# An encoder layer in split fp32: all instructions recorded and issued in a planned order, 8 KB tiles in shared places, whole-block operand parts, six of eight pairs in seven products

## The chip, the cores and the metric

The kernel runs on one core of one Trainium2 chip. The metric is the device time of one execution in microseconds (us), and the median of several runs counts. A core has a matrix engine (TensorE, "PE" in the profile; "PEld" is its weight load), a vector engine (VectorE, "DVE"), a scalar engine (ScalarE, "ACT"), GpSimd ("POOL") and a sync engine ("SP") that here only issues DMAs. Each engine works its own instructions off in order and waits on semaphores for the others. Matmuls write to PSUM, eight banks of 128 x 512 fp32; everything else lies in SBUF, 128 partitions wide.

## The reference

One encoder layer for 256 tokens of width 2048, in fp32:

```python
x = x + 0.5 * swiglu(rmsnorm(x, ffn1_norm), ffn1_w_gate, ffn1_w_up, ffn1_w_down)
h = rmsnorm(x, mix_norm)
proj = h @ w_in                          # pool | q | k | v | q_mem | gate logits, 12800 columns
gates = sigmoid(proj[..., c5:] + b_gate)
y_pool = pooling_branch(u_pool, pool_w, pool_scale) @ w_up_pool
y_attn = dilated_attention_branch(q, k, v, positions) @ w_up_attn
y_mem = memory_branch(q_mem, rmsnorm(mem, mem_norm), w_mem_kv) @ w_up_mem
merged = gates_0 * y_pool + gates_1 * y_attn + gates_2 * y_mem
x = x + merged @ w_out
x = x + 0.5 * swiglu(rmsnorm(x, ffn2_norm), ffn2_w_gate, ffn2_w_up, ffn2_w_down)
return rmsnorm(x, final_norm)
```

`swiglu(x, g, u, d)` is `(silu(x @ g) * (x @ u)) @ d` with 5632 hidden columns. The two FFNs hold most of the weights.

## The kernel before

**Split fp32.** Every fp32 operand is split into a high part (rounded to the matrix engine's fp32r format by a ScalarE copy, line 112) and a low part (the rest, by a VectorE subtraction, line 113). A product of two blocks takes three matmuls: low x high, high x high, high x low (lines 207 to 209 in `gemm`, 232 to 234 in `pair_gemm`, 597 to 599 in the down products). Each has a stationary block of 128 x 128 (the activations) and a moving block of 128 x 512 (the weights).

**Weights.** `weights` (line 130) loads four 128-row blocks of 512 columns in one DMA of 1 MB into a tile `wf` (three of them). `kept` (line 121) splits it in two halves of two blocks: one ACT copy and one DVE subtraction of 128 x 1024 for each half, into the 4 KB tiles `wh` and `wl`, of which there are six each. `pair_weights` does the same for a pair of row blocks of the gate matrix (`n` = 0) and of the up matrix (`n` = 1), in two DMAs of 512 KB; for the first pair of the first chunk it loads and splits block by block (`piece` = 1).

**The FFN.** `ffn` goes over 11 chunks of 512 hidden columns (`up(c)`). A chunk multiplies the 16 row blocks of the width, as eight *pairs* j = 0 to 7, with the gate and the up matrix. A pair is a 2 x 2 block product: two token blocks by two row blocks, times two row blocks by (gate, up). Done plainly it takes eight products (`EIGHT_PRODUCTS`); with sums of blocks on both sides it takes seven (`SEVEN_PRODUCTS`, a Strassen-Winograd scheme). `SEVEN = (1, 2, 3, 5, 6)` lists the pairs that do; in chunk 0 none do, in chunk 1 those in `SEVEN[1::2]` (2 and 5), in chunks 2 to 10 all five, and these come first in the chunk. A seven-product pair needs sums of weight blocks: three VectorE additions (lines 155 to 157; the first is 128 x 1024), then a split of the four sums (lines 160 and 161), and its own three blocks are split too (`kept(wf, 3)`). It needs sums of the activation blocks as well, once per FFN, from `fill_pair`. The products add up in one PSUM bank each, and `finish` combines them when the last pair is done.

From chunk 2 on, the down product of chunk c - 2 is put between the seven-product products: eight pieces of 12 matmuls (`down_pieces`), one PSUM bank, then an ACT copy to a tile `y` (line 601, two `half` places, shared with other small tiles) and a POOL DMA that adds `y` to x in DRAM (line 602, `accum_op`). The down products of the last two chunks are done as plain gemms at the end, and x is loaded back by `x_chunk` (line 546).

**The middle.** After FFN 1 come plain gemms (`gemm`, two sets of two PSUM banks in turn) for the memory keys, values and queries, the pooling input, the gates, q, k, v, the up projections and `w_out`, with the small work of the branches put between them.

**What sets the order.** The program itself is written in the order wanted: `queue` holds small pieces of work (transposes, splits, activations), and `pop` sets some of them in after each product. Each engine's instructions then follow that writing order as the tile framework schedules it, with waits where a tile's place isn't free yet. SP issues nearly all loads, in order, and POOL the stores of x.

**Memory.** A pool of 14 `slot` places of 8 KB (per partition) holds operands, sums and the larger tiles; beside it lie three `wf` of 8 KB, six `wh` and six `wl` of 4 KB. An FFN's activations take five `seven` tiles and two shared `lhs` tiles for the other three pairs.

**The start.** SP issues the loads of the transposed x (`load_x`, 256 KB a pair) between those of the weights. Nine idle matmuls warm TensorE. For pair 1 (`SUMS = {5: 1}`) the sums of activation blocks are made later, before pair 5 of chunk 1 (`late_sums`); for the other seven-product pairs at once.

Of the kernel before, what the change touches and what calls it, by code (L numbers as in the profile page):

```python
# [9 lines left out]
F32 = mybir.dt.float32  # L10
# [32 lines left out]
SEVEN = (1, 2, 3, 5, 6)  # L43
SUMS = {5: 1}
# [21 lines left out]

@with_exitstack
def tile_encoder_layer(ctx: ExitStack, tc: tile.TileContext, a: dict, out: bass.AP):
    nc = tc.nc
    sb = ctx.enter_context(tc.tile_pool(name="sb", bufs=1))  # L70
    ps = ctx.enter_context(tc.tile_pool(name="ps", bufs=1, space=bass.MemoryType.PSUM))
    dr = ctx.enter_context(tc.tile_pool(name="dr", bufs=1, space=bass.MemoryType.DRAM))
# [6 lines left out]
    def slot(shape, dtype=F32, name="slot"):  # L79
        return sb.tile(shape, dtype, tag="slot", bufs=14, name=nm(name))  # L80
# [49 lines left out]
    def weights(w, row, col):  # L130

        wf = sb.tile([P, 4, CW], F32, tag="wf", bufs=3, name=nm("wf"))
# [3 lines left out]
    def pair_weights(w, cols, j, seven, piece=2, beside=()):  # L136


        wf = sb.tile([P, 4, CW], F32, tag="wf", bufs=3, name=nm("wf"))
        beside = list(beside)  # L140
        halves = [operands() for _ in range(2)] if piece < 2 else None
        for n in range(2):
            block = w[n][cols[n] // CW, j // 2].rearrange("p (k c) -> p k c", k=4)
            for k in range(0, 2, piece):
# [4 lines left out]
                if piece < 2:  # L149
                    wh, wl = halves[n]  # L150
                    split(wh[:, k : k + 1], wl[:, k : k + 1], wf[:, r])
        if not seven:
            return halves or kept(wf, 4)
# [29 lines left out]
    def gemm(lhs, w, row, col, last=False, sets=((0, 1), (2, 3))):  # L183
# [10 lines left out]
        for pairs in order:  # L194
            for kb, t in pairs:
# [7 lines left out]
                wh, wl = W[kb // 4][kb // 2 % 2]  # L203
# [3 lines left out]
                nc.tensor.matmul(parts[t], lo, wh[:, k % 2], start=kb == 0, stop=False)  # L207
                nc.tensor.matmul(parts[t], hi, wh[:, k % 2], start=False, stop=False)  # L208
                nc.tensor.matmul(parts[t], hi, wl[:, k % 2], start=False, stop=kb == n - 1)  # L209
# [13 lines left out]
    def pair_gemm(lhs, w, cols, order, sevens, out, after_seven=(), before=None, pieces=None, between=()):  # L223
# [12 lines left out]
        def block(W, b):  # L236

            wh, wl = W[min(b // 2, 2)]
            i = b - 4 if b >= 4 else b % 2
            return wh[:, i], wl[:, i]  # L240
# [938 lines left out]
```

## Time and profile before

| what | value |
|---|---|
| median of 3 runs (lowest to highest) | 2348.73 us (2348.28 to 2348.74) |
| profiled execution | 2348.81 us, span 2347.0 us |
| TensorE clock granted, mean | 0.999 |
| VectorE, FFN chunks (140 to 620 us) | 419.59 us busy of 480 |
| ScalarE, the same | 295.73 us busy of 480 |
| DMA, the same | 77% of the 16 engines, 227 GB/s |
| VectorE, the middle (740 to 1600 us) | 594.08 us busy of 860 |

The span goes from the first to the last instruction; the execution's time has 1.8 us around it. A row of the grouped view names line, engine, operation, tiles (out <- in), shape and count; then the total busy time, the mean of one, and the idle time of the engine just before these instructions with what ended it. A row of the timeline begins with the start and the duration in us, and "x2" joins neighbours; what stands in brackets is idle time before it and its releaser. A window's row gives, for PE, PEld, DVE, ACT and POOL, busy us and (instructions), then the clock, the DMA share and GB/s.

### The profile page before, as it was taken

How to read it: one execution, taken by the hardware profiler on the slowest of the kernel's cores; microseconds unless marked ns; L12 is line 12 of the kernel's file. 1: busy time of each engine (PE TensorE's matmuls, PEld its weight loads, DVE VectorE, ACT ScalarE, POOL GpSimd, SP SyncE). 2: the span in 40 equal slices, each digit the busy share in tenths (PEclk: the TensorE clock that was granted, in tenths of full speed). 3: DMA queues.
4: the chain of work that ended last, by engine and by line, in shares of the span. 5: the costliest groups of instructions: out<-in, count | busy, mean ns of one | idle time of the engine just before them, and what ended most of it. 6: DMA issues, size and time to landing. Idle time of an engine off the chain costs nothing.

```text
span 2347.0 us, 27962 instructions
## 1 busy us (share of the span) xinstructions
PE 2334.9 (99%) x10271; PEld 1877.0 (80%) x10271; DVE 1827.2 (78%) x2218; ACT 1311.8 (56%) x1609; POOL 138.5 (6%) x174
## 2 busy tenths in 40 slices
PE   9999999999999999999999999999999999999998
PEld 7888888888888888888888888887887888888886
DVE  7988888889867676757777656876698988888875
ACT  8565666666566445543334454455566666565654
POOL 0011111111100000000000000000011111111110
PEclk9999999999999999999999999999999999999999
DMA  8687878777786545555545455566577777777883
GB/s 327 207 237 217 248 229 236 222 228 223 229 294 223 197 180 198 188 199 187 188 180 197 171 173 189 202 218 207 195 213 226 229 228 225 229 220 223 245 253 147
DMA packets 119033, 506.27 MB, mean 216 GB/s; under 512 B 13680, under 2 KB 14960, under 8 KB 87664
## 3 DMA queue, kind: packets, MB, share of 16 engines
q1 hardware_dynamic: 95952, 459.39, 56.7%
q0 software_dynamic: 22656, 44.05, 10.7%
q8 instruction: 80, 1.31, 0.2%
q10 hardware_dynamic: 288, 1.05, 0.1%
q14 instruction: 57, 0.47, 0.1%
HBM read 458.30 MB, written 46.14 MB: 215 GB/s over the span
## 4 chain that ended last, share of the span: by engine, by line
PE 99%; DMA 0%; DVE 0%; SPq 0%; ACT 0%; issue 0%; DVEq 0%; ACTq 0%
PE acc L208 13%; PE acc L207 13%; PE acc L209 13%; PE q L232 13%; PE q L233 13%; PE q L234 13%; PE down L598 6%; PE down L599 6%; PE down L597 6%; PE bank L396 1%; PE bank L877 0%; PE bank L803 0%; PE bank L768 0%; DMA wf<-in_ffn_w_gate 0%; PE bank L861 0%; PE bank L1027 0%
## 5 line engine op out<-in xcount | busy, mean ns | idle before, releaser
L113 DVE TENSOR_TENSOR wl<-wf,wh 128x1024 fp32r<-128x1024 f32 (+1 forms) x834 | 951.9, 1159 | 362.8 <-ACT wh L112 358.8
L112 ACT ACTIVATE wh<-wf 128x1024 fp32r<-128x1024 f32 (+1 forms) x834 | 837.1, 1009 | 702.9 <-PE acc L208 406.1
L207 PE MATMUL acc<-wh,lhs 128*128 128x512 f32 x1344 | 537.7, 400 | 0.0
L208 PE MATMUL acc<-wh,lhs 128*128 128x512 f32 x1344 | 534.3, 398 | 0.0
L209 PE MATMUL acc<-wl,lhs 128*128 128x512 f32 x1344 | 528.4, 393 | 0.0
L207 PEld LDWEIGHTS acc<-wh,lhs 128*128 128x128 f32 x1344 | 252.5, 188 | 64.7 <-DVE lhs L113 0.3
L209 PEld LDWEIGHTS acc<-wl,lhs 128*128 128x128 f32 x1344 | 252.3, 188 | 60.6
L208 PEld LDWEIGHTS acc<-wh,lhs 128*128 128x128 f32 x1344 | 252.7, 188 | 54.3
L160 ACT ACTIVATE sumsh<-sums 128x1024 fp32r<-128x1024 f32 x188 | 197.0, 1055 | 105.9 <-DVE sums L157 58.3
L161 DVE TENSOR_TENSOR sumsl<-sums,sumsh 128x1024 fp32r<-128x1024 f32 x188 | 228.1, 1220 | 11.2 <-ACT sumsh L160 10.3
L598 PE MATMUL down<-wh,lhs 128*128 128x512 f32 x576 | 228.5, 397 | 0.0
L599 PE MATMUL down<-wl,lhs 128*128 128x512 f32 x576 | 228.0, 396 | 0.0
L597 PE MATMUL down<-wh,lhs 128*128 128x512 f32 x576 | 227.5, 395 | 0.0
L232 PE MATMUL q<-wh,lhs 128*128 128x512 f32 x528 | 222.1, 421 | 2.1 <-ACT wh L112 2.1
L233 PE MATMUL q<-wh,lhs 128*128 128x512 f32 x528 | 208.3, 395 | 0.0
L234 PE MATMUL q<-wl,lhs 128*128 128x512 f32 x528 | 208.2, 395 | 0.0
L602 POOL DMA_DIRECT2D x<-y x144 | 124.6, 865 | 1156.6 <-ACT y L601 1136.3
L232 PE MATMUL q<-wh,seven 128*128 128x512 f32 x410 | 163.9, 400 | 0.0
L234 PE MATMUL q<-wl,seven 128*128 128x512 f32 x410 | 162.5, 397 | 0.0
L601 ACT ACTIVATE y<-down 128x512 f32<-128x512 f32 x144 | 85.3, 592 | 138.1 <-PE down L599 79.7
L233 PE MATMUL q<-wh,seven 128*128 128x512 f32 x410 | 162.0, 395 | 0.0
L233 PE MATMUL q<-sumsh,seven 128*128 128x512 f32 x376 | 148.7, 395 | 0.0
(174 smaller groups left out, 2551.7 us busy)
## 6 DMA issues: line engine op xcount, KB each, us to landing
wf<-in_w_in SPq DMA_DIRECT2D x100, 1024.0 KB, 4.8
wf<-in_ffn_w_down SPq DMA_DIRECT2D x88, 1024.0 KB, 5.3
wf<-in_ffn_w_gate SPq DMA_DIRECT2D x175, 512.0 KB, 5.3
wf<-in_ffn_w_up SPq DMA_DIRECT2D x175, 512.0 KB, 6.7
x<-y POOLq DMA_DIRECT2D x144, 256.0 KB, 6.4
wf<-in_w_mem_kv SPq DMA_DIRECT2D x16, 1024.0 KB, 5.2
wf<-in_w_out SPq DMA_DIRECT2D x16, 1024.0 KB, 4.8
wf<-in_w_up_pool SPq DMA_DIRECT2D x8, 1024.0 KB, 4.8
```

The source lines that it names most:

```text
L112: nc.scalar.activation(hi, src, AF.Copy)
L113: nc.vector.tensor_sub(lo, src, hi.bitcast(F32))
L161: nc.vector.tensor_sub(tl[:, r], sums[:, r], th[:, r].bitcast(F32))
L207: nc.tensor.matmul(parts[t], lo, wh[:, k % 2], start=kb == 0, stop=False)
L208: nc.tensor.matmul(parts[t], hi, wh[:, k % 2], start=False, stop=False)
L209: nc.tensor.matmul(parts[t], hi, wl[:, k % 2], start=False, stop=kb == n - 1)
L232: nc.tensor.matmul(Q[q], lhsl, wh, start=first, stop=False)
L233: nc.tensor.matmul(Q[q], lhsh, wh, start=False, stop=False)
L234: nc.tensor.matmul(Q[q], lhsh, wl, start=False, stop=final)
L597: nc.tensor.matmul(b, lo, wh[:, k % 2], start=k == 0, stop=False)
L598: nc.tensor.matmul(b, hi, wh[:, k % 2], start=False, stop=False)
L599: nc.tensor.matmul(b, hi, wl[:, k % 2], start=False, stop=k == 3)
```

## The change

1. Every instruction is recorded first (`Recorder`, `Plan.record`), with its tiles, the parts of them that it reads and writes, and an assumed cost. At the end `Plan.issue` plays the program through with these costs: each engine takes, of the instructions whose inputs are ready, the one recorded earliest whose tiles have a place (`room`); SP and POOL keep the recorded order. The instructions are then issued in the order found, and each tile has the place that the play gave it.
2. All 8 KB tiles (`slot`, `wf`, `wh`, `wl`) share 23 places.
3. Operand parts are four blocks wide: `kept` splits a weight tile in one ACT and one DVE instruction. The four sums' low parts are one DVE instruction too; their high parts stay two ACT copies.
4. `SEVEN = (1, 2, 3, 4, 5, 6)`. Chunk 1 has pairs 2, 4 and 6 in seven products, chunks 2 to 10 six pairs. In FFN 1 all sums of activation blocks are made later: their record index is shifted to 220 (pairs 2, 4, 6) or 400 (pairs 1, 3, 5).
5. The loads of `x_chunk`, `mem`, `memT`, `inv_count`, `pool_w`, `b_gate` and `mask` are issued by POOL instead of SP.

The diff, cut to its core (`View` stands for a tile or a part of one and notes slicing and reshaping; `View.bits` gives the cells that it covers):

```diff
-SEVEN = (1, 2, 3, 5, 6)
-SUMS = {5: 1}
+SEVEN = (1, 2, 3, 4, 5, 6)
+SUMS = (220, 400)
...
+    def record(self, engine, name, args, kw):
...
+        for view, writes in [(v, False) for v in views] + [(v, True) for v in outs]:
+            t, bits = view.tile, view.bits()
+            tiles[id(t)] = t
+            for other, theirs, wrote in t.log:
+                chained = engine == other.engine == "tensor"
+                if other is not w and (theirs & bits and (writes or wrote) or chained and writes and wrote):
+                    before.add(other)
...
+        w.index = len(self.works) + self.shift
+        self.works.append(w)
...
+    def cost(self, engine, name, out, views, kw):
+        if name == "dma_start":
+            return (60, 0) if engine != "gpsimd" else (860, 0)
+        n = max(v.free() for v in [out, *views] if isinstance(v, View))
+        if engine == "tensor":
+            if name == "transpose":
+                return 111, 160
+            n = out.free()
+            dtype = views[0].dtype
+            if dtype == F32:
+                return 0.84 * 2 * n, 160
+            return (n * 17 / 16 + 16 if dtype == F32R else n) / 2.4, 160
+        if engine == "vector":
+            if name == "transpose":
+                return 180 + n, 30
+            return (210 if name == "scalar_tensor_tensor" else 160) + 1.042 * n, 30
+        if engine == "scalar":
+            return 210 + 0.834 * n + (50 if any(v.free() <= 2 for v in views) else 0), 30
+        return 500, 100
+
+    def issue(self):
...
+        def room(w):
+            need = {}
+            for t in w.tiles:
+                if t.placed is None:
+                    need.setdefault(id(t.group), (t.group, []))[1].append(t)
+            for group, tiles in need.values():
+                first = min(t.rank for t in tiles)
...
+                earlier = sum(t.placed is None for t in group.tiles[group.next : first])
+                if len(group.free) - earlier < len(tiles):
+                    return False
+            return True
...
+            for e in engines:
+                while free_at[e] <= now and able[e]:
+                    skipped, w = [], None
+                    if e in turn and able[e][0][0] != turn[e][0]:
+                        break
+                    while able[e] and len(skipped) < (1 if e in turn else 24):
+                        item = heapq.heappop(able[e])
+                        if room(item[1]):
+                            w = item[1]
+                            break
+                        skipped.append(item)
...
+                    end = now + w.cost
+                    if w.link and w.link != link:
+                        link = w.link
+                        end += 1283
+                    free_at[e] = end
+                    done = end + w.lag
+                    if w.bytes:
+                        hard = e != "gpsimd"
+                        lines = max(end + (1300 if hard else 2000), lines) + w.bytes / (190 if w.adds else 365)
+                        done = lines + (600 if hard else 1000)
+                    order.append(w)
...
+        with self.tc.manual_schedule():
+            for w in order:
+                w.call()
...
-        return sb.tile(shape, dtype, tag="slot", bufs=14, name=nm(name))
+        return sb.tile(shape, dtype, tag="slot", bufs=23, name=nm(name))
...
     def operands():
-        return [sb.tile([P, 2, CW], F32R, tag=tag, bufs=6, name=nm(tag)) for tag in ("wh", "wl")]
+        return [slot([P, 4, CW], F32R, name) for name in ("wh", "wl")]
 
     def kept(wf, n):
-        halves = [operands() for _ in range(2)]
-        for i, (wh, wl) in enumerate(halves):
-            m = min(2, n - 2 * i)
-            split(wh[:, :m], wl[:, :m], wf[:, 2 * i : 2 * i + m])
-        return halves
+        wh, wl = operands()
+        split(wh[:, :n], wl[:, :n], wf[:, :n])
+        return wh, wl
...
-        wf = sb.tile([P, 4, CW], F32, tag="wf", bufs=3, name=nm("wf"))
+        wf = sb.tile([P, 4, CW], F32, tag="slot", bufs=23, name=nm("wf"))
...
         for r in (slice(0, 2), slice(2, 4)):
             nc.scalar.activation(th[:, r], sums[:, r], AF.Copy)
-            nc.vector.tensor_sub(tl[:, r], sums[:, r], th[:, r].bitcast(F32))
-        return *kept(wf, 3), (th, tl)
+        nc.vector.tensor_sub(tl, sums, th.bitcast(F32))
+        return kept(wf, 3), (th, tl)
...
+            def rest():
+                straight(1)
+                with nc.shifted(max(0, sums_at - nc.now())):
+                    own(0)
+                    own(1)
+                    sums()
+                    parts(slice(4, 8))
+
+            return [lambda: straight(0), rest]
...
-        fill = fill_pair(lhs1[j], lambda: xt, g_ffn1[:, 2 * j : 2 * j + 2], own_only=j in SUMS.values())
+        fill = fill_pair(lhs1[j], lambda: xt, g_ffn1[:, 2 * j : 2 * j + 2], SUMS[j not in SEVEN[1::2]])
...
-            nc.sync.dma_start(out=xs[:, t], in_=XD[n][t])
+            nc.gpsimd.dma_start(out=xs[:, t], in_=XD[n][t])
...
-        nc.sync.dma_start(
+        nc.gpsimd.dma_start(
             out=bg, in_=a["b_gate"][:, i * D + n * CW : i * D + (n + 1) * CW].partition_broadcast(P)
         )
...
+    nc.issue()
```

More of the change, by code (lines that the diff above doesn't have):

```diff
@@ L1 @@
-from contextlib import ExitStack
+from contextlib import ExitStack, contextmanager
 import numpy as np
@@ new lines, with __init__, place @@
+class Whole:
+    def __init__(self, make, group, shape):
+        self.make, self.group, self.shape = make, group, shape
+        self.whole, self.made, self.users, self.log = None, None, 0, []
+        self.placed = None
+    def place(self):
+        if self.made is None:
+            self.made = self.make(self.placed)
+        return self.made
+class Group:
+    def __init__(self, places):
+        self.free, self.tiles, self.next = list(range(places)), [], 0
+class Work:
+    def __init__(self, engine, call, cost, lag):
+        self.engine, self.call, self.cost, self.lag = engine, call, cost, lag
+        self.waits, self.then, self.ready, self.tiles, self.link = 0, [], 0.0, (), 0
+        self.bytes, self.adds = 0, False
@@ L136, in pair_weights @@
     def pair_weights(w, cols, j, seven, piece=2, beside=()):
-        wf = sb.tile([P, 4, CW], F32, tag="wf", bufs=3, name=nm("wf"))
+        wf = sb.tile([P, 4, CW], F32, tag="slot", bufs=23, name=nm("wf"))
         beside = list(beside)
-        halves = [operands() for _ in range(2)] if piece < 2 else None
+        parts = operands() if piece < 2 else None
         for n in range(2):
@@ L149, in pair_weights @@
                 if piece < 2:
[L150 to L151 removed]
+                    split(parts[0][:, r], parts[1][:, r], wf[:, r])
         if not seven:
[L153 removed]
+            return (parts or kept(wf, 4),)
         sums = slot([P, 4, CW], F32, "sums")
@@ L360, in fill_pair, with own, sums, parts @@
             return [lambda k=k: part(k) for k in range(2)]
-        if own_only:
+        F = []
+        def own(k):
+            if not F:
+                F.append(tmp([P, 8, P], "blocks"))
+            nc.scalar.activation(
+                F[0][:, 2 * k : 2 * k + 2], src()[:, k].rearrange("p (t c) -> p t c", t=T), AF.Copy, scale=gain[:, k : k + 1]
+            )
+        def sums():
+            nc.vector.tensor_sub(F[0][:, 4], F[0][:, 3], F[0][:, 1])
+            nc.vector.tensor_sub(F[0][:, 5], F[0][:, 2], F[0][:, 3])
+            nc.vector.tensor_sub(F[0][:, 6], F[0][:, 2], F[0][:, 4])
+            nc.vector.tensor_sub(F[0][:, 7], F[0][:, 0], F[0][:, 6])
+        def parts(r):
+            split(L[:, 0, r], L[:, 1, r], F[0][:, r])
+        if sums_at is not None:
             def straight(k):
@@ L557, in up @@
             opening = c == 0 and first is not None
-            kw = dict(before=first[0], pieces=lambda j: 1 if j == 0 else 2) if opening else {}
-            if c == 1 and first is not None:
-                kw = dict(before=first[1])
+            kw = dict(before=first, pieces=lambda j: 1 if j == 0 else 2) if opening else {}
             out = []
@@ L693, in load @@
                 rows[t] = slot([P, D], F32, "mem")
-                nc.sync.dma_start(out=rows[t], in_=a["mem"][t * P : (t + 1) * P, :])
+                nc.gpsimd.dma_start(out=rows[t], in_=a["mem"][t * P : (t + 1) * P, :])
             else:
                 columns[n] = tmp([P, 4, S], "xt")
-                nc.sync.dma_start(out=columns[n], in_=a["memT"][:, 4 * n : 4 * n + 4, :])
+                nc.gpsimd.dma_start(out=columns[n], in_=a["memT"][:, 4 * n : 4 * n + 4, :])
         def squares(t, n):
@@ L945, in tile_encoder_layer @@
     mask = v2[:, 1]
-    nc.sync.dma_start(out=mask, in_=a["mask"])
+    nc.gpsimd.dma_start(out=mask, in_=a["mask"])
     for g in range(3):
```

234 lines of the change are left out of this document (191 added, 43 removed).

## The prediction

> **What bounds the kernel now.** I read the page first: busy times, then the chain that ended last.
>
> ```profile
> span 2347.0 us, 27962 instructions
> PE 2334.9 (99%) x10271; PEld 1877.0 (80%) x10271; DVE 1827.2 (78%) x2218; ACT 1311.8 (56%) x1609; POOL 138.5 (6%) x174
> PE 99%; DMA 0%; DVE 0%; SPq 0%; ACT 0%; issue 0%; DVEq 0%; ACTq 0%
> L207 PE MATMUL acc<-wh,lhs 128*128 128x512 f32 x1344 | 537.7, 400 | 0.0
> L598 PE MATMUL down<-wh,lhs 128*128 128x512 f32 x576 | 228.5, 397 | 0.0
> L232 PE MATMUL q<-wh,lhs 128*128 128x512 f32 x528 | 222.1, 421 | 2.1 <-ACT wh L112 2.1
> L232 PE MATMUL q<-wh,seven 128*128 128x512 f32 x410 | 163.9, 400 | 0.0
> L233 PE MATMUL q<-sumsh,seven 128*128 128x512 f32 x376 | 148.7, 395 | 0.0
> ```
>
> The chain is TensorE for 99%. "Busy" is no proof, because matmuls overlap (0.40 us listed each), so I take the step from one start to the next out of the timeline of an FFN chunk.
>
> ```profile
> 199.64 0.39 PE L597 MATMUL down<-wh,lhs 128*128 128x512 f32 x1
> ...
> 208.49 0.39 PE L234 MATMUL q<-wl,lhs 128*128 128x512 f32 x1
> 208.72 0.27 PE L396 MATMUL bank<-ident,up 128*128 128x128 f32 x1
> ...
> 209.30 0.39 PE L234 MATMUL q<-wl,lhs 128*128 128x512 f32 x1
> ```
>
> From 199.64 to 208.49 lie 38 steps: 8.85 / 38 = 0.233 us for a 512-column matmul. From 208.49 to 209.30 there are three matmuls and one transpose: 0.81 - 0.70 = 0.11 us for the transpose. Each of the five groups above stands once in each of the three lines of its triple, so there are 3 x (1344 + 576 + 528 + 410 + 376) = 9702 such matmuls, and 9702 x 0.233 = 2261 us. That leaves 86 us of the span for 569 small matmuls (some 0.12 us each: 68 us) and about 18 us for start and tail. So the sum closes with next to no waiting in between: only fewer matmuls, a shorter start or a shorter tail can make it faster, and any stall makes it slower. The start and the tail:
>
> ```profile
> 5.55 0.51 PE L232 MATMUL q<-wh,lhs 128*128 128x512 f32 x1 [0.67 <-ACT wh L112]
> ...
> 6.59 0.62 PE L234 MATMUL q<-wl,lhs 128*128 128x512 f32 x2
> 8.68 0.50 PE L232 MATMUL q<-wh,lhs 128*128 128x512 f32 x1 [1.47 <-ACT wh L112]
> ...
> 9.50 0.41 PE L234 MATMUL q<-wl,lhs 128*128 128x512 f32 x1
> ...
> 12.78 0.39 PE L234 MATMUL q<-wl,lhs 128*128 128x512 f32 x1
> 13.01 0.40 PE L232 MATMUL q<-wh,seven 128*128 128x512 f32 x1
> ```
> ```profile
> 11.56 1.06 ACT L112 ACTIVATE wh<-wf 128x1024 fp32r<-128x1024 f32 x1 [0.35 <-DMA wf<-in_ffn_w_gate]
> 12.81 1.06 ACT L112 ACTIVATE wh<-wf 128x1024 fp32r<-128x1024 f32 x1 [0.18 <-DMA wf<-in_ffn_w_up]
> ```
> ```profile
> 2338.36 0.69 DVE L616 SCALAR_TENSOR_TENSOR xs<-acc,xs 128x512 f32<-128x512 f32 x1
> ```
>
> The first real matmul starts at 5.55; two starts at 6.59 and 6.82 are followed by one at 8.68, a hole of 8.68 - 6.82 - 0.23 = 1.6 us in which the second gate piece is awaited. Pair 1 begins at 13.01, without a hole behind pair 0. The tail, from L616 at 2338.36 to the end, is 8.6 us.
>
> **The change, part by part.**
>
> *Products.* A pair in seven products saves one product of three matmuls. Before, each FFN has 2 such pairs in chunk 1 and 5 in each of chunks 2 to 10: 47, twice 94, which the count below (x94) confirms. After it has 3 and 6: 57, twice 114. Twenty products go, 60 matmuls x 0.233 = **14.0 us**, all of it on the chain. For the vector engine it means more work, below.
>
> *Operand parts four blocks wide.* One ACT and one DVE instruction in place of two. VectorE at saturation, and the widths on both engines:
>
> ```profile
> 212.51 1.22 DVE L155 TENSOR_TENSOR sums<-wf 128x1024 f32<-128x1024 f32 x1
> 213.65 0.68 DVE L113 TENSOR_TENSOR lhs<-bank,lhs 128x512 fp32r<-128x512 f32 x1
> 214.25 0.68 DVE L156 TENSOR_TENSOR sums<-sums,wf 128x512 f32<-128x512 f32 x1
> ```
> ```profile
> L155 DVE TENSOR_TENSOR sums<-wf 128x1024 f32<-128x1024 f32 x94 | 114.6, 1220 | 5.9 <-DMA wf<-in_ffn_w_up 5.8
> L112 ACT ACTIVATE wh<-wf 128x1024 fp32r<-128x1024 f32 x736 | 775.9, 1059 | 673.0 <-PE acc L208 406.1 <-PE q L233 145.9 <-PE down L598 63.1
> L112 ACT ACTIVATE wh<-wf 128x512 fp32r<-128x512 f32 x98 | 61.9, 631 | 29.8 <-PE down L598 10.5 <-PE q L233 7.6 <-ACT gate L572 6.8
> ```
>
> Back to back a 1024-wide VectorE step takes 1.14 us (212.51 to 213.65) and a 512-wide one 0.60. The step per 512 is 0.54, so 2048 should take 2.22 and 1536 1.68: a merged pair saves only 0.06 us there. [...] On ScalarE 1059 - 631 = 428 ns per 512 gives 1.06 + 0.86 = 1.92 us for 2048. In steady state both lie beside the matmuls and cost nothing; the cover is what was prepared ahead. At the start there is no cover. Chunk 0's pairs from the second on are split whole: the split waits for the up half too (landed when ACT takes it at 12.81), then needs 1.92 us, so pair 1 can begin at about 14.8 and not at 13.01: 1.8 us. Its low parts come 2.3 us after that (2.22 and a hand-over), while the four banks can take two matmuls each meanwhile (8 x 0.233 = 1.9): another 0.3 or so. From pair 2 on, a pair is 24 x 0.233 = 5.6 us of matmuls against 1.92 and 2.22 us, and the split is ahead. I take **+2.0 us**. Bounds: below, -1.6, if the new order closes the hole before 8.68; above, +3.8, if the planned order runs each triple to its end, so that the 1.9 us of filling is lost too.
>
> *Order and places.* `Plan.issue` lays every engine's order out from assumed costs; SP and POOL stay in recorded order. Work lacks nothing now, so a better order has only the hole at 8.68 to win, and a wrong one has everything to lose. The 14 slots, 3 `wf` and 12 half-size parts were 184 KB; 23 shared places are the same. I take 0, with the rivals for the upper bound.
>
> *Loads moved from SP to POOL* (`x_chunk`, `mem`, `memT`, `inv`, `pool_w`, `bg`, `mask`). They pass the accumulating stores in POOL's queue:
>
> ```profile
> x<-y POOLq DMA_DIRECT2D x144, 256.0 KB, 6.4
> ...
> xs<-x SPq DMA_DIRECT2D x24, 256.0 KB, 5.3
> ```
> ```profile
> 2299.03 0.80 SPq L546 DMA_DIRECT2D xs<-x  x2
> ...
> 2306.17 1.39 DVE L616 SCALAR_TENSOR_TENSOR xs<-acc,xs 128x512 f32<-128x512 f32 x2
> ```
>
> Of equal size, POOL's take 1.1 us longer, and two of them follow each other, so a chunk of x may come 1 to 3 us later against 7.1 us from issue to first use; the sums wait in PSUM behind it, of which gemms have two sets in turn. I take 0; without that cover it would be up to 3 us in each of 12 places. In exchange, weights no longer queue behind these waits on SP. The tail's instructions are the same: 0, within half a microsecond either way.
>
> *Sum.* The profiled run took 2348.81 us, the runs' median is 2348.73, so it stands for them. 2348.8 - 14.0 + 2.0 = **2336.8 us**.
>
> **Rivals.**
>
> *VectorE becomes the bound in the seven-product phase* (slower). Six pairs at 1.14 + 2 x 0.60 + 2.22 + 1.68 = 6.24 give 37.4 us, four down blocks 4 x 2.22 = 8.9, twelve narrow steps 7.2: 53.5 us, while TensorE has (42 x 3 + 96) x 0.233 = 51.7 us there. If nothing is prepared ahead, 1.8 us are lost in each of 18 chunks: 32 us, so 2369. It is slower than before once more than 12 / 18 = 0.7 us per chunk stays uncovered. The windows of such a chunk speak about it:
>
> ```profile
> 212.00:256.00 44.00, 44.00 (x192) 35.36 (x191) 43.36 (x49) 28.54 (x35) 3.96 (x5) 1.00 0.78 239
> 256.00:271.00 15.00, 15.00 (x66) 12.07 (x65) 8.72 (x10) 7.35 (x10) 2.09 (x3) 1.00 0.86 244
> 140.00:620.00 480.00, 480.00 (x2093) 385.01 (x2092) 419.59 (x459) 295.73 (x350) 49.53 (x58) 1.00 0.77 227
> ```
>
> VectorE (third pair of columns) already works 43.4 of 44 us in that phase, then idles 6 of 15. By the same prices the present phase needs 31.8 + 9.1 + 7.2 = 48.1 us in 201 x 0.233 = 46.8: a deficit of 1.3, which TensorE doesn't feel. After, the eights phase leaves 12.1 - 4.4 = 7.7 us to work ahead, and the mean load goes from 419.6 / 480 = 87% to about 93%. So it is closer, but places, shared by all, should cover 1.8 us. Chance 0.10.
>
> *ScalarE held at `y`* (same or slower). The copy of a down block into one of two `half` places waits for an accumulating store; behind it in ACT's queue stand the weight splits, and for those TensorE waits.
>
> ```profile
> ACT y L601 <- DMA x<-y: 22.6, 18, 3.2
> ```
>
> The plan counts 860 + 2000 + 1380 + 1000 ns for such a store, 5.2 us, against the 6.4 above. If the 22.6 us reached TensorE in whole it would be 2359, half of it 2348. Against it: TensorE feels none of this now, and down blocks come further apart (42 products for eight of them, not 35). Chance 0.09.
>
> *The start costs nothing* and its hole closes: 2348.8 - 14.0 - 1.6 = 2333.2. Against it: the hole waits on a landing that no order changes. Chance 0.06.
>
> *The clock falls at the new hole at the start.* A hole of 1.8 us could send TensorE back to the rate at which it warmed up:
>
> ```profile
> L323 PE MATMUL idle<-idle 128*128 128x512 bf16 x9 | 3.6, 576 | 1.3 <-DVE idle L320 1.3
> ```
>
> Another 3.6 us at half rate would lose 1.8: 2338.6. Against it: after the 1.6 us hole the step from 9.50 to 12.78 is 3.28 / 14 = 0.234, full speed. Chance 0.03. [...]
>
> **How the numbers follow.** Forecast 0.72, VectorE 0.10, `y` 0.09, cheap start 0.06, clock 0.03. The range takes in the bounds of the start (2348.8 - 14.0 with -1.6 and +3.8: 2333.2 to 2338.6), half a microsecond of tail, and the lower third of the `y` case, up to 2345; it leaves out VectorE and most of `y`. A measurement tells about 0.2% (4.7 us) from no change. Faster: 0.72 + 0.06 + 0.03 and 0.02 of `y`: 0.83. Same: 0.05, slower 0.12.
>
> **What the changed profile would show.** Right: 60 matmuls fewer in the groups of the FFN lines, sums x114, the step still 0.233; a start of pair 1 near 14.8 with a hole before it on ACT's split; VectorE near 93% in the FFN windows and TensorE's starts unbroken there. Wrong: TensorE rows with idle time put down to `wl`, `sumsl` or `wh` in chunks 2 to 10 (the VectorE rival), ACT waits at `y` above 22.6 us with TensorE idle beside them, or holes at a gemm's start behind a POOL load.

## The result and the profile after

| | before | after |
|---|---|---|
| median of the runs, us | 2348.73 (2348.28 to 2349.04) | 2307.43 (2305.32 to 2309.57) |
| ratio, 95% interval | | 0.9824, 0.9807 to 0.9841 |
| profiled execution, us (span) | 2348.81 (2347.0) | 2307.88 (2306.1) |

The change saves 41 us where 12 were forecast. The page of the changed kernel (every line is L225 now, the line at which the recorder calls an instruction, so groups go by tiles):

```profile
span 2306.1 us, 26456 instructions
PE 2286.4 (99%) x10211; PEld 1866.8 (81%) x10211; DVE 1871.0 (81%) x1805; ACT 1270.7 (55%) x1244; POOL 163.6 (7%) x221
PE 56%; issue 35%; POOL 4%; DMA 2%; DVE 2%; ACT 1%; SPq 0%; POOLq 0%; DVEq 0%; ACTq 0%
L225 PE MATMUL acc<-wh,lhs 128*128 128x512 f32 x2688 | 842.0, 394 | 0.0
L225 DVE TENSOR_TENSOR sumsl<-sums,sumsh 128x2048 fp32r<-128x2048 f32 x114 | 260.5, 2285 | 15.3 <-ACT sumsh L225 15.0
```

Sixty matmuls fewer (10271 to 10211) and sums x114, as forecast. TensorE still fills 99% of the span. So the missing 29 us are not waits that went; each matmul got shorter. Matmuls overlap, so their listed length tells little (400 ns became 394); what tells is how many start in a stretch without a gap. The windows view of the same 100 us of gate gemms, before and after (the pair behind the stretch and its length is PE's busy time and its count):

```profile
1080.00:1180.00 100.00, 100.00 (x431) 80.42 (x430) 77.64 (x116) 39.43 (x38) 0.00 (x0) 1.00 0.50 183
```
```profile
1080.00:1180.00 100.00, 100.00 (x441) 82.31 (x440) 78.17 (x102) 33.46 (x19) 0.00 (x0) 1.00 0.50 175
```

In 100 us at the full granted clock (the 1.00) TensorE does 441 matmuls instead of 431, in the same stage with the same products. In the timeline of the changed kernel:

```profile
1149.66 0.39 PE L225 MATMUL acc<-wl,lhs 128*128 128x512 f32 x1
1149.89 0.61 PE L225 MATMUL acc<-wh,lhs 128*128 128x512 f32 x2
...
1152.38 0.39 PE L225 MATMUL acc<-wl,lhs 128*128 128x512 f32 x1
```

From 1149.66 to 1152.38 are 12 steps: 0.2267 us each, where the kernel before took 0.233. (In the formula of the plan's `cost`, which counts in 1/2.4 ns, these are 544 and 560 counts.) Over all starts of the trace that are less than 290 ns apart the step is 233.3 ns before and 228.9 after. That closes the sum from the first matmul's start to the last one's, 2336.6 us before and 2295.8 after:

- 60 matmuls fewer, at 233.3 ns: -14.0
- 4.33 ns less on the 9651 of 512 columns that are left: -41.8
- longer gaps between matmuls of 512 columns (26.0 us over the step before, 38.5 after): +12.5
- small matmuls and the gaps at them: +2.5

Together -40.8. The largest new gaps are the one at the start that was forecast, and one at 695 us, which was not. Of the changed kernel, TensorE, then ScalarE and VectorE at the start:

```profile
12.32 0.39 PE L225 MATMUL q<-wl,lhs 128*128 128x512 f32 x1
14.66 2.75 PE L225 MATMUL q<-wh,seven 128*128 128x512 f32 x8 [1.96 <-ACT wh L225]
```
```profile
12.70 1.91 ACT L225 ACTIVATE wh<-wf 128x2048 fp32r<-128x2048 f32 x1 [1.73 <-DMA wf<-in_ffn_w_up]
```
```profile
14.64 2.29 DVE L225 TENSOR_TENSOR wl<-wf,wh 128x2048 fp32r<-128x2048 f32 x1 [3.08 <-ACT wh L225]
```

The up half lands, one split of 1.91 us follows, and pair 1 begins at 14.66 (forecast: about 14.8). At 695 us TensorE waits for VectorE's `lhs`, and that for ScalarE, which stands in order at a `mem` load:

```profile
695.15 0.40 PE L225 MATMUL acc<-wl,lhs 128*128 128x512 f32 x1
698.25 0.44 PE L225 MATMUL bank<-ident,xs 128*128 128x128 f32 x2 [2.70 <-DVE lhs L225]
```
```profile
694.64 0.63 ACT L225 ACTIVATE junk<-mem 128x512 bf16<-128x512 f32 x1 [2.95 <-DMA mem<-in_mem]
```

Behind both gaps the granted clock (third column from the end) falls to half for one stretch of 3.4 us, in which eight matmuls, at the second gap seven, take 427 ns each: some 1.6 us lost each time. The first gap:

```profile
14.66:15.90 1.24, 1.24 (x5) 1.05 (x6) 1.24 (x1) 1.24 (x4) 0.00 (x0) 1.00 1.06 416
15.93:19.34 3.41, 3.41 (x10) 2.53 (x8) 3.41 (x6) 3.10 (x5) 0.00 (x0) 0.50 1.02 410
19.34:21.00 1.66, 1.66 (x9) 1.35 (x8) 1.66 (x3) 1.66 (x5) 1.25 (x2) 1.00 1.05 410
```

### The profile page after: what moved, and what is told of

Its sections match the earlier page's. It is cut to its first block, busy times and chain, and to the rows that moved or that the text cites. A ratio compares the mean times of both kernels' runs of the same rounds, so it can differ in the third digit from the quotient of the medians.

```text
span 2306.1 us, 26456 instructions
## 1 busy us (share of the span) xinstructions
PE 2286.4 (99%) x10211; PEld 1866.8 (81%) x10211; DVE 1871.0 (81%) x1805; ACT 1270.7 (55%) x1244; POOL 163.6 (7%) x221
## 4 chain that ended last, share of the span: by engine, by line
PE 56%; issue 35%; POOL 4%; DMA 2%; DVE 2%; ACT 1%; SPq 0%; POOLq 0%; DVEq 0%; ACTq 0%
PE acc L225 39%; PE q L225 12%; POOL x L225 4%; PE down L225 3%; PE bank L225 2%; DMA x<-y 1%; DVE wl L225 1%; DMA mem<-in_mem 1%; DMA wf<-in_ffn_w_up 0%; DMA xt<-in_memT 0%; ACT wh L225 0%; DVE sums L225 0%; DVE lhs L225 0%; SPq L225 0%; ACT junk L225 0%
## 5 line engine op out<-in xcount | busy, mean ns | idle before, releaser
L225 DVE TENSOR_TENSOR wl<-wf,wh 128x2048 fp32r<-128x2048 f32 (+2 forms) x419 | 885.0, 2126 | 162.3 <-ACT wh L225 121.3
L225 ACT ACTIVATE wh<-wf 128x2048 fp32r<-128x2048 f32 (+2 forms) x419 | 741.4, 1783 | 305.9 <-PE acc L225 108.8
L225 PE MATMUL acc<-wh,lhs 128*128 128x512 f32 x2688 | 842.0, 394 | 0.0
L225 PEld LDWEIGHTS acc<-wh,lhs 128*128 128x128 f32 x2688 | 498.0, 188 | 107.3
L225 PE MATMUL acc<-wl,lhs 128*128 128x512 f32 x1344 | 525.5, 392 | 0.4 <-DVE wl L225 0.4
L225 PE MATMUL down<-wh,lhs 128*128 128x512 f32 x1152 | 359.2, 391 | 0.0
L225 PE MATMUL q<-wh,seven 128*128 128x512 f32 x972 | 303.4, 393 | 4.0 <-DVE lhs L225 2.0
L225 ACT ACTIVATE sumsh<-sums 128x1024 fp32r<-128x1024 f32 x228 | 237.1, 1057 | 117.2 <-DVE sums L225 117.2
L225 PEld LDWEIGHTS acc<-wl,lhs 128*128 128x128 f32 x1344 | 252.6, 188 | 56.0 <-DVE wl L225 1.1
L225 PE MATMUL q<-sumsh,seven 128*128 128x512 f32 x912 | 274.5, 391 | 0.0
L225 DVE TENSOR_TENSOR sumsl<-sums,sumsh 128x2048 fp32r<-128x2048 f32 x114 | 260.5, 2285 | 15.3 <-ACT sumsh L225 15.0
L225 PEld LDWEIGHTS down<-wh,lhs 128*128 128x128 f32 x1152 | 216.3, 188 | 47.6
L225 PE MATMUL q<-wh,lhs 128*128 128x512 f32 x704 | 232.2, 411 | 1.0 <-ACT wh L225 1.0
L225 ACT ACTIVATE y<-down 128x512 f32<-128x512 f32 x144 | 86.4, 600 | 254.8 <-PE down L225 141.8
L225 PE MATMUL down<-wl,lhs 128*128 128x512 f32 x576 | 225.4, 391 | 0.0
L225 PEld LDWEIGHTS q<-wh,seven 128*128 128x128 f32 x972 | 182.3, 189 | 46.3 <-PE q L225 4.8
L225 POOL DMA_DIRECT2D x<-y x144 | 123.9, 860 | 1133.1 <-ACT y L225 1126.1
L225 PEld LDWEIGHTS q<-sumsh,seven 128*128 128x128 f32 x912 | 171.2, 188 | 37.4
L225 PE MATMUL q<-wl,seven 128*128 128x512 f32 x486 | 190.0, 392 | 0.0
L225 DVE TENSOR_TENSOR sums<-sums,wf 128x512 f32<-128x512 f32 x228 | 157.8, 692 | 7.7
L225 PE MATMUL q<-sumsl,seven 128*128 128x512 f32 x456 | 163.6, 391 | 0.0
L225 PEld LDWEIGHTS q<-wh,lhs 128*128 128x128 f32 x704 | 120.2, 189 | 32.4 <-ACT wh L225 2.5
```

Of the source, the lines that this page charges most:

```text
L225: return getattr(getattr(self.nc, engine), name)(*map(real, args), **{k: real(v) for k, v in kw.items()})
```

## The experiments

### Where the shorter step comes from

The built programs show where the tiles lie in a partition. Before: `one` (padded to 32 bytes), the 14 slots of 8 KB from byte 16544, `gains` (288 bytes), and behind it wf, wh (from 158720) and wl. After: all operands in 23 places of 8 KB, 21 of them in a row from 17344, the last two 32 bytes off that grid (from 197600). In both kernels a tile's blocks are cut at multiples of 512 bytes. The first theory was that a start that is no multiple of 64 bytes costs time (theory A); the rival, that order, wide parts or VectorE's load do it (theory B). Three kernels first:

Experiment 1, the kernel before with two pads:

```diff
-    one = sb.tile([P, 1], F32, name="one")
+    one = sb.tile([P, 9], F32, name="one")[:, :1]
...
-    gains = sb.tile([P, 4 * KB + 8], F32, name="gains")
+    gains = sb.tile([P, 4 * KB + 16], F32, name="gains")
...
```

> The kernel before, with 32 bytes of padding behind `one` and 32 behind `gains`, so that every operand of a matmul starts at a multiple of 64 bytes in its partition (in the kernel before, the operands held in `slot` start 32 bytes off such a multiple, and wf, wh and wl on one). Not one instruction is added, taken away or moved. Theory A (the step of a 512-column matmul depends on the start addresses of its two operands modulo 64 bytes): the step falls from 233.3 to 226.7 ns, as in the aligned stretches of the changed kernel, on about 9700 matmuls, so about 64 us less, 2284 us, or some us above that where VectorE or ScalarE then no longer keeps up. Theory B (the recorded order, the wide parts or the fewer VectorE instructions made the step smaller): no address changes anything, 2348.7 us with a step of 233.3 ns.

Experiment 2, the first pad alone:

> The kernel before with the 32 bytes of padding behind `one` alone: the operands in `slot` now start at a multiple of 64 bytes, and wf, wh and wl, which lie behind them, 32 bytes off one. Still one of the two operands of nearly each matmul is off. Theory A, in the form that one operand off costs as much whichever it is: a step of 233.3 to 233.6 ns, 2344 to 2349 us (the matmuls on sums, both of whose operands are in slots, gain). Theory A, in the form that only the stationary operand counts: 226.7 ns, about 2285 us. Theory B: 2348.7 us.

Experiment 3, the second alone:

> The kernel before with the 32 bytes behind `gains` alone: both operands of each matmul now start 32 bytes off a multiple of 64. Theory A, with the step of 230.4 to 231.1 ns that the stretches show in which both operands are off: 2320 to 2327 us. If a second operand off cost as much again as the first, the step would be 240 ns and the time about 2410 us. Theory B: 2348.7 us.

Measured: 2337.97 us (ratio 0.9955, 0.9941 to 0.9969), 2348.85 (1.0001, 0.9992 to 1.0010) and 2338.16 (0.9955, 0.9941 to 0.9969). Theory B falls, since 32 bytes of padding move the time by 10.7 us; theory A falls too, since all on 64 bytes gave 2338 and not 2284, and all off gave the same. What experiments 1 and 3 have in common is the *distance* of wh and wl from the slots, 384 bytes modulo 512; before and in experiment 2 it is 352. In the changed kernel it is 0 for most pairs of operands. That is theory A2, and it has a test. Experiment 5, with 160 bytes behind `gains`, makes it 0:

```diff
-    gains = sb.tile([P, 4 * KB + 8], F32, name="gains")
+    gains = sb.tile([P, 4 * KB + 48], F32, name="gains")
...
```

> The kernel before with 160 bytes of padding behind `gains`, so that wf, wh and wl lie at the same residue modulo 512 bytes as the slots (in the kernel before they lie 352 bytes off it, and in the first experiment 384). Nothing else changes; both operands are now 32 bytes off a multiple of 64. Theory A2 (what counts is not each address but the distance of the moving operand from the stationary one modulo 512 bytes; in the changed kernel 21 of its 23 places lie at the same residue, and the step is 226.7 ns): step 226.7 to 228 ns, 2284 to 2300 us. Theory A (each address modulo 64 by itself): 2338 us, as the third experiment. Theory B (order, wide parts, VectorE's load): 2348.7 us.

Experiment 6 has 32 bytes behind `one` as well:

> As the run before it, with 32 bytes behind `one` as well: the same distances (0 modulo 512), and both operands at a multiple of 64 bytes, as in the changed kernel. Theory A2: as the run before it within 2 us, 2284 to 2300 us. If both the distance and the 64-byte start count, this one alone reaches 226.7 ns (2284 to 2290 us) and the run before it doesn't. Theory B: 2348.7 us.

Experiment 7 has 416 bytes behind `gains`:

> The kernel before with 416 bytes behind `gains`: the distance of wh and wl from the slots is 256 modulo 512. Theory A2 with 512 bytes as the period: a step of 230 to 233 ns, 2320 to 2348 us. With 256 bytes as the period (128 is excluded by the first experiment's distance of 384, whose step was 232.1 ns): 226.7 to 228 ns, 2284 to 2300 us. Theory B: 2348.7 us.

Experiment 8 breaks the grid of the changed kernel:

```diff
+                def make(place):
+                    if (tag, place) == ("slot", 11) and not plan.padded:
+                        plan.padded.append(real.tile([128, 40], F32, tag="pad", bufs=1, name="pad"))
+                    return real.tile(shape, dtype, tag=f"{tag or name}_{place}", bufs=1, name=name)
...
```

> The changed kernel with 160 bytes laid between its eleventh and twelfth place, so that a matmul whose operands lie on both sides of that border has a distance of 160 or 352 bytes modulo 512; which places they share, the order and every instruction stay. Theory A2: about half of the pairs of operands are now at unlike residues and break up the even stretches, so the step goes from 228.9 to 231 to 233.3 ns, 20 to 42 us more: 2327 to 2350 us. Theory B: the changed kernel's 2307.4 us.

Measured: 2294.41 us (0.9770, 0.9755 to 0.9784), 2295.16 (0.9773, 0.9757 to 0.9789), 2296.12 (0.9776, 0.9761 to 0.9790) and 2333.93 (0.9937, 0.9922 to 0.9952). The same 100 us in experiments 1, 5, 7 and 8:

```profile
1080.00:1180.00 100.00, 100.00 (x432) 81.06 (x431) 80.59 (x124) 39.35 (x38) 0.00 (x0) 1.00 0.51 187
```
```profile
1080.00:1180.00 100.00, 100.00 (x442) 82.79 (x442) 75.44 (x109) 41.60 (x41) 0.00 (x0) 1.00 0.54 199
```
```profile
1080.00:1180.00 100.00, 100.00 (x443) 82.84 (x442) 75.60 (x109) 41.34 (x41) 0.00 (x0) 1.00 0.55 202
```
```profile
1080.00:1180.00 100.00, 100.00 (x433) 81.03 (x432) 75.09 (x105) 32.63 (x19) 0.00 (x0) 1.00 0.50 176
```

So theory A2 holds, with 256 bytes as the period: at a distance of 0 or 256 the step is 227.3 ns, at 384 it is 232.2, at 352 it is 233.3 (means over the starts of each trace). Padding alone takes 54 us off the kernel before, and 160 bytes in the midst of the changed kernel's places take back 26.5 of its 41. Of other distances only 96 and 128 modulo 256 were measured, each between the slots and `wh`/`wl` of a whole kernel.

Two things the kept traces settle beyond this. A pad moves all that lies behind it, so the other engines' reads and writes and the DMAs could have been what got in the way. But in the kernel before 26 matmuls lie in stretches in which no DMA packet was under way and no other engine worked (0.3 us on either side taken in), and their step is 233.4 ns; in experiment 5 it is 226.7. And the distance isn't a price of each matmul by itself. The matmuls on sums have both operands in slots, at a distance of 0 in the kernel before too, yet nine of them in a row are slow there (the first and the last of nine, before, then in experiment 5):

```profile
236.91 0.39 PE L232 MATMUL q<-sumsh,seven 128*128 128x512 f32 x1
...
238.76 0.39 PE L234 MATMUL q<-sumsl,seven 128*128 128x512 f32 x1
```
```profile
232.60 0.39 PE L232 MATMUL q<-sumsh,seven 128*128 128x512 f32 x1
...
234.41 0.39 PE L234 MATMUL q<-sumsl,seven 128*128 128x512 f32 x1
```

Eight steps take 1.85 us before and 1.81 in experiment 5; over all 922 starts from one matmul on sums to the next the step is 231.7 and 226.7 ns. So what is shown is that it matters how the operand tiles of a kernel lie to each other; a matmul whose own two operands lie well is slow among others that lie badly. Nothing here shows why.

Experiment 9 puts the changed kernel's last two places on the grid:

```diff
-        junk = half_tmp([P, CW], BF16, "junk")
+        junk = half_tmp([P, CW + 624], BF16, "junk")[:, :CW]
...
-        return sb.tile([P, T, NCH], F32, tag="ssq", bufs=2, name=nm("ssq"))
+        return sb.tile([P, 2 * T, NCH], F32, tag="ssq", bufs=2, name=nm("ssq"))[:, :T]
```

> The changed kernel with its last two places moved up by 480 bytes (a wider tile for `junk`, a longer one for `ssq`, whose added parts nothing reads), so that all 23 start at the same residue modulo 512. Theory A2: step from 228.9 to 227.2 ns on 9400 matmuls, 16 us less than the changed kernel, 2291 us; and then it stands only some 3 us below the kernel before with the padding alone (2294.4). Theory B: 2307.4 us.

2293.15 us (0.9765, 0.9750 to 0.9780). At equal steps the whole rest of the change, the sixth pair with it, is worth 1.3 us against experiment 5, which the spread of the runs doesn't tell from nothing.

### What the rest of the change does

Experiment 4, the kernel before with the sixth pair and nothing else:

```diff
-SEVEN = (1, 2, 3, 5, 6)
+SEVEN = (1, 2, 3, 4, 5, 6)
```

> The kernel before with pair 4 of the eight in seven products as well (SEVEN = 1 to 6), nothing else. Both theories: 60 matmuls fewer of 233.3 ns, 14.0 us less, 2334.7 us, if VectorE's added splits and sums stay hidden. If they don't (the rival of the prediction in which VectorE becomes the bound), over 2345 us.

Experiment 13, the same on experiment 5:

> The fifth experiment's kernel (before, padded by 160 bytes, 2294.4 us) with pair 4 in seven products as well. By the products' term alone: 60 x 227.3 ns = 13.6 us less, 2280.8 us. By the fourth experiment, where the same edit cost 5 us in place of saving 14 since VectorE came late in the old order (holes of 46.0 us in sum against 24.7): at the shorter step VectorE is later still, so 5 to 15 us more, 2299 to 2310 us. If the latter, the sixth pair is what the made order buys.

2353.74 us (1.0017, 1.0008 to 1.0026) in place of 2334.7, and 2314.41 (0.9855, 0.9839 to 0.9871) in place of 2280.8: in the old order the sixth pair costs 5 and 20 us, 19 and 34 more than the products alone would give, and more than the 5 to 15 us that experiment 13 was expected to lose. In experiment 13 TensorE stands in nearly each chunk; its waits (us in total, times, longest one), and VectorE's and TensorE's timelines at one such place:

```profile
PEld q L234 <- DVE sumsl L161: 19.3, 24, 1.0
PEld q L232 <- ACT sumsh L160: 14.7, 24, 1.2
```
```profile
2018.22 1.22 DVE L155 TENSOR_TENSOR sums<-wf 128x1024 f32<-128x1024 f32 x1
2019.36 1.22 DVE L161 TENSOR_TENSOR sumsl<-sums,sumsh 128x1024 fp32r<-128x1024 f32 x1
2020.49 0.69 DVE L156 TENSOR_TENSOR sums<-sums,wf 128x512 f32<-128x512 f32 x1
```
```profile
2019.65 0.40 PE L233 MATMUL q<-wh,seven 128*128 128x512 f32 x1
2020.63 0.49 PE L234 MATMUL q<-sumsl,seven 128*128 128x512 f32 x1 [0.58 <-DVE sumsl L161]
```

From 2015.87 on VectorE goes without a pause, and `sumsl` is late. That looks like the prediction's first rival, but VectorE had just stood still itself. Ahead of these rows ScalarE waited for a gate load, and VectorE for ScalarE's `sumsh` behind it:

```profile
2013.83 1.06 ACT L112 ACTIVATE wh<-wf 128x1024 fp32r<-128x1024 f32 x1 [2.55 <-DMA wf<-in_ffn_w_gate]
```
```profile
2015.87 1.23 DVE L161 TENSOR_TENSOR sumsl<-sums,sumsh 128x1024 fp32r<-128x1024 f32 x1 [1.50 <-ACT sumsh L160]
```

It is so at all 35 places from 20 us on at which a matmul on sums starts over 0.42 us behind the one ahead of it (21.0 us together): within the 8 us before, VectorE had stood for `sumsh` for 0.48 us or more. ScalarE's waits for gate loads are 48.4 us in experiment 13, and 6.7 in experiment 5:

```profile
ACT wh L112 <- DMA wf<-in_ffn_w_gate: 48.4, 28, 4.5
```
```profile
ACT wh L112 <- DMA wf<-in_ffn_w_gate: 6.7, 8, 1.4
```

So VectorE isn't full here; in the old order, with three `wf` places, gate loads come too late for the sixth pair, and the wait goes from ScalarE, mostly over VectorE, to TensorE. In the made order the same load finds room. Of experiment 13, of the changed kernel, and of experiment 9, whose step is that of experiment 13 (third pair of columns: VectorE):

```profile
140.00:620.00 480.00, 473.52 (x2096) 383.99 (x2095) 451.87 (x502) 310.08 (x371) 51.78 (x60) 1.00 0.82 231
```
```profile
140.00:620.00 480.00, 478.51 (x2116) 388.80 (x2115) 450.67 (x368) 297.50 (x282) 51.61 (x60) 1.00 0.79 233
```
```profile
140.00:620.00 480.00, 477.35 (x2130) 391.71 (x2129) 453.81 (x372) 300.45 (x285) 52.42 (x61) 1.00 0.79 236
```

VectorE is busy alike, 94%, but TensorE lacks 6.5 us of 480 in the first, 1.5 in the second and 2.7 in the third. Whether it is the order or the shared places that holds the loads in time was not tried apart. Experiment 12 takes the sixth pair out of experiment 9:

> The ninth experiment's kernel with five pairs in seven products instead of six: 60 matmuls more, 20 sums fewer to split. By the prediction's first term, at this step: 60 x 227.2 ns = 13.6 us more than the ninth experiment's kernel, about 2305 us. If VectorE's load is a bound in the made order too, less than that is lost, 2291 to 2300 us.

2306.79 us (0.9824, 0.9807 to 0.9840), 13.6 more, as the products say. But with the same five pairs and the same step, experiment 5 takes 2294.4: the made order, with the wide parts and the moved loads that go with it, loses 12.4 us. Experiments 10 and 11, on experiment 9, undo the two suspects that the trace shows:

```diff
-        parts = operands() if piece < 2 else None
+        parts = operands() if piece < 2 or beside else None
...
-                if piece < 2:
+                if parts:
```

> The run before it with chunk 0's blocks split two at a time again (parts two blocks wide for the first chunk alone). The prediction's start term said that a part four blocks wide holds pair 1 back by 2 us; the trace has the hole from 12.3 to 14.7 us and, behind it, 8 matmuls at half the step's speed (1.6 us). If that is its cause: 3 to 4 us less than the run before it, 2287 to 2288 us. If something else opens the hole: within 1 us of it.

```diff
-            nc.gpsimd.dma_start(out=xs[:, t], in_=XD[n][t])
+            nc.sync.dma_start(out=xs[:, t], in_=XD[n][t])
```

(and so for the six other moved loads)

> The ninth experiment's kernel with the moved loads (xs, mem, memT, inv_count, cumT, the band's and the mask) issued by SP again, as in the kernel before. The prediction costed this move at nothing; the trace shows a hole at 695 us in which ScalarE waits 2.95 us for the `mem` load, with 8 matmuls at half speed behind it. If the move opened it: 3 to 5 us less than the ninth experiment's kernel, about 2287 us. If the order made in the kernel opened it (which sets the load's turn from an assumed time): within 1 us of it.

2291.36 us (0.9756, 0.9741 to 0.9771) and 2299.27 (0.9788, 0.9773 to 0.9802): 1.8 us less where 3 to 4 were expected, and 6.1 more where 3 to 5 less, or no change, were. The start's gap did close in experiment 10, where pair 1 begins at once:

```profile
12.06 0.39 PE L225 MATMUL q<-wl,lhs 128*128 128x512 f32 x1
12.28 1.07 PE L225 MATMUL q<-wh,seven 128*128 128x512 f32 x4
```

but gaps of 1.0 to 1.4 us at 51, 57 and 102 us came instead. With the plans as made, the loads are better on POOL. Any edit makes the plan anew, so an edit of one place moves gaps elsewhere. So the plan's own assumptions were tried, each alone on experiment 9 (14 and 15), then both on experiment 10 (16):

```diff
-            return (n * 17 / 16 + 16 if dtype == F32R else n) / 2.4, 160
+            return (n * 17 / 16 if dtype == F32R else n) / 2.4, 160
```

> The ninth experiment's kernel (2293.2 us) whose plan costs a matmul of 512 columns at 544 cycles of 2.4 GHz (226.7 ns) in place of 560 (233.3 ns); only the order that the plan makes changes. If the holes of 0.7 to 1.4 us at the borders of the chunks (221.6, 347.3, 472.6, 598.0, 1863.7, 1988.9, 2114.1 us) come from a plan that thinks PE slower than it is: 4 to 6 us less, 2287 to 2289 us. If they come from something else: within 2 us of 2293.2.

```diff
-                        lines = max(end + (1300 if hard else 2000), lines) + w.bytes / (190 if w.adds else 365)
+                        lines = max(end + (1300 if hard else 4500), lines) + w.bytes / (190 if w.adds else 365)
```

> The ninth experiment's kernel whose plan takes loads issued by POOL to land 2.5 us later than before (the `mem` load took 10.0 us from issue to landing by the trace; the plan assumed about 7). If the hole at 695 us (2.1 to 2.9 us and 8 matmuls at half speed behind it, 1.6 us) comes from this assumed time: 3 to 5 us less, 2288 to 2290 us. If not: within 2 us of 2293.2.

> The tenth experiment's kernel (2291.4 us) with both of the plan's times changed, as in the two runs before this one. If both sources of holes are as supposed: 7 to 10 us less than the tenth, 2281 to 2284 us, the fastest so far. If the holes only move: 2289 to 2294 us.

2288.82 us (0.9746, 0.9731 to 0.9761), 2293.12 (0.9765, 0.9750 to 0.9779) and 2297.23 (0.9782, 0.9767 to 0.9796). The true step is worth 4.3 us, where 4 to 6 were expected. Of the seven steps of 0.70 to 1.35 us that experiment 9 has at the chunk borders none is left, and the longest between two matmuls of 512 columns from 20 us on is 0.65. But its gap of 2.5 us at 691 us is gone too, with the fall of the clock behind it, so not all of the 4.3 is shown to come from the borders. The later landing (experiment 15), from which 3 to 5 us were expected, brought nothing: it closed the gap at 695 us and opened 3 us of others at 917 us; with both times and the narrow first chunk the time grew, by 5.9 us over experiment 10, so the gaps only moved. Last, experiment 14 with five pairs (17), and with weights split two blocks at a time (18):

> The fourteenth experiment's kernel (2288.8 us) with five pairs in seven products. By the products alone 13.6 us more: 2302.4 us, 8 us above the kernel before with its padding (2294.4). If the plan's wrong step was the whole of what the made order lost, the time is near 2294 us, and the sixth pair is worth only 5 us.

```diff
-        split(wh[:, :n], wl[:, :n], wf[:, :n])
+        for r in (slice(0, 2), slice(2, n)):
+            split(wh[:, r], wl[:, r], wf[:, r])
```

> The fourteenth experiment's kernel whose splits of weights are done two blocks at a time again (two ACT and two DVE instructions for a part, tiles unchanged, still six pairs). If the wide instructions cost only the start hole (2.36 us at 12.5 us): 2 to 3 us less, 2286 to 2287 us. If the saved starts of instructions matter where VectorE is at 94% of the span (the prediction has 0.06 us a part): 419 parts, some 25 us more work for VectorE and 60 for ScalarE, of which a part gets through: 2290 to 2300 us.

2300.23 us (0.9795, 0.9778 to 0.9813) and 2296.50 (0.9776, 0.9761 to 0.9792). With the mended plan the made order at five pairs still loses 5.8 us to experiment 5, and what holds it there was not settled. The wide instructions are worth 7.7 us at six pairs: without them TensorE waits again, in experiment 18 for

```profile
PEld q L225 <- ACT sumsh L225: 12.5, 15, 3.0
```

Here VectorE is the one that comes late: ahead of 13 of these 15 waits (all from 171 us on) ScalarE stood 5.8 us for VectorE's `sums`, and VectorE had no pause over 0.25 us in the 6 us before. The longest, at 96 us, has a fall of the clock behind it.

Experiment 14 is the fastest kernel of all, 60 us below the one before.

## Why the prediction was wrong, step by step

**The step that failed: "Order and places ... 23 shared places are the same. I take 0", and with it the named sign "the step still 0.233".** The places hold as many bytes as before, but they lie differently to each other. The prediction took 0.233 us out of the timeline as the price of a matmul, though it was the price in a kernel whose moving weights lie 96 bytes, modulo 256, from the stationary blocks. There was a sign that could have been asked about: the idle matmuls at the start, 512 columns too, start 427 ns apart, as the changed kernel's do at half the granted clock, and half of 427 is 213, 20 below the step. The step alone is -41.8 us where the whole is -40.8; experiments 5 and 8 show it in both directions.

**Products, -14.0: right.** Sixty matmuls went, and experiment 12 prices sixty at 13.6 us with the shorter step.

**Wide parts, +2.0 at the start: right in size and place.** Pair 1 began at 14.66 in place of 13.01. Elsewhere they were costed at nothing beside the matmuls; in the made order they are a gain, 7.7 us by experiment 18, in which VectorE, busy 459.55 us of 480 (140 to 620 us; 453.81 in experiment 9), comes late at the chunk borders.

**Order, 0: wrong in both directions.** "A better order has only the hole at 8.68 to win" holds for five pairs, where the made order lost 12.4 us. For six pairs it was the condition for the product term: 2293.2 us against 2314.4 in the old order, whose loads came late. The prediction asked what the new order wins on the old work, and not what the old order would do with the new work.

**Moved loads, 0: near.** One gap at 695 us hangs on a POOL load, but on SP the time is 6.1 us longer (experiment 11).

**Tail, 0: right.** From the last `xs` step to the end 8.5 us, before 8.6:

```profile
2297.57 0.69 DVE L225 SCALAR_TENSOR_TENSOR xs<-acc,xs 128x512 f32<-128x512 f32 x1
```

**The rivals.** *VectorE the bound*: its load was forecast at 93% and is 93.9% (450.67 of 480 us), and it did not bind after the change. Its price of 32 us looks like the 34 of experiment 13, but that is luck: at the step that the prediction reckoned with, the old order lost 19 us (experiment 4), and in both VectorE stood waiting behind a late load. The rival itself shows in experiment 18, with narrow parts. *ScalarE held at `y`*: didn't come. The wait for the store is gone from ScalarE's rows, which now wait for the product itself (another 104.7 us have no releaser in the profile):

```profile
ACT y L225 <- PE down L225: 141.8, 74, 4.4
```

*The clock falls at the new hole* (chance 0.03): it did in this trace, for 1.6 us against the 1.8 forecast, and a second time at 695 us; in experiments 8, 12, 14, 15 and 17 the same hole at the start is there and the clock stays. *The start free*: didn't come.

By its own terms the prediction thus had the products and the start right, lacked 41.8 us of the step, and lacked some 15 us of gaps that the made order opened; the start's 2.0 is part of these.

## What to carry to other kernels

Before costing an edit in matmuls, compare the step with half of what the same matmul takes at half the granted clock (here half of 427, 213 ns, against a step of 233): if it is well above that in a stream without gaps, look at where the operand tiles start, and pad so that all of them lie multiples of 256 bytes apart; here 160 bytes were worth 54 us (233 to 227 ns). A change that moves tiles moves this distance by accident, so measure at equal addresses before giving the credit to the order or to the work saved. And an edit that saves the bound engine's work has to be costed together with the order that will carry it: the same sixth pair lost 20 us in one order and won 13.6 in the other. An engine that runs without a pause ahead of a wait need not be the bound: look some microseconds further back for what held it.

## What the runs showed of the hardware

In a stream of 512-column fp32r matmuls the step is 227.3 ns on the mean when all operand tiles lie multiples of 256 bytes from each other in each partition (experiments 5 to 7 and 9). With the moving weights 128 bytes off the stationary blocks, modulo 256, it is 232.2 (experiments 1 and 3), at 96 it is 233.3 (the kernel before), and there matmuls whose own two operands lie well are slow among the others (231.7, and 226.7 in experiment 5). Where both start modulo 64, at 32 or at 0, made no difference (2294.4 us in experiment 5 against 2295.2 in experiment 6).

In these traces the granted clock fell after gaps much shorter than the 3.41 us for which it then stayed low. In the profiles of the changed kernel and of experiments 4 to 18 there are 16 stretches of over 2 us between two starts of matmuls; 9 were followed by seven or eight matmuls at 427 ns, 7 were not. The shortest with a fall is 2.25 us (experiment 10, at 688 us), the longest without one 3.35 us (experiment 8), so the length alone doesn't decide. (In experiments 11 and 16 the clock also fell behind groups of gaps of 1.3 to 1.6 us.) That gap of experiment 8, and the granted clock of 1.00 in what follows it:

```profile
701.28 0.40 PE L230 MATMUL acc<-wl,lhs 128*128 128x512 f32 x1
...
704.63 0.44 PE L230 MATMUL bank<-ident,xs 128*128 128x128 f32 x2 [2.95 <-DVE lhs L230]
```
```profile
702.00:708.00 6.00, 3.37 (x16) 2.79 (x17) 2.69 (x7) 5.98 (x14) 1.08 (x2) 1.00 0.90 341
```

In these traces it is the place in time that tells the two apart. In each trace every change of the clock between its first rise and the end of the matmuls lies a whole number of times 3.413 us behind that rise (in the changed kernel the rise is at 5.66 us, the changes at 15.90, 19.32, 698.57 and 701.98). Cut into such stretches, the 20 traces have 11 with a fall at their end, and in each of these TensorE had stood for 2.10 us or more, its gaps (what lies between two starts beyond a step) taken together; in none of the 13412 others did it stand longer than 2.03. The gap of experiment 8 falls on two stretches, 1.87 us in one and 1.48 in the other. The stretches of the changed kernel ahead of its two falls, then these two of experiment 8:

```profile
12.49:15.90 3.41, 1.45 (x6) 1.05 (x6) 1.25 (x1) 3.20 (x5) 0.00 (x0) 1.00 1.01 401
695.16:698.57 3.41, 0.71 (x5) 0.33 (x4) 1.36 (x3) 3.41 (x12) 0.00 (x0) 1.00 1.01 408
```
```profile
699.87:703.28 3.41, 1.81 (x9) 1.16 (x7) 0.16 (x1) 2.26 (x7) 0.08 (x1) 1.00 1.00 411
703.28:706.70 3.42, 2.07 (x10) 1.76 (x11) 2.01 (x6) 3.42 (x9) 0.47 (x1) 1.00 0.88 329
```
